# A hybrid bidirectional encoder on one core: scan products moved from GpSimd to VectorE, attention's one-column operations in per-row scalar form, output weights split in quarters

## The chip, the cores and the metric

The kernel runs on one core of a Trainium2 chip. A core has TensorE (matmuls; PE in the profile, PEld for its weight loads), VectorE (DVE), ScalarE (ACT), GpSimd (POOL) and SyncE (SP, which here only issues DMAs), and 16 DMA engines between SBUF and device memory. Each engine works through its own instructions in order and meets the others only at semaphores. The metric is the device time of the program in microseconds (us); lower is better.

## The reference, cut to what matters

Two layers over a sequence of 2048 rows of 1024 numbers. A layer normalises, projects to 4128 columns, feeds three head groups, gates each, concatenates, projects back and adds the residual:

```python
for layer in range(DEPTH):                      # DEPTH = 2
    h = rms_norm(x, norm_pre[layer])
    proj = h @ w_in[layer]
    y_a = gla_branch(...)    # gated linear attention, both directions
    y_b = diff_branch(...)   # differential softmax attention, 4 heads
    y_c = hgrn_branch(...)   # gated linear recurrence, both directions
    y = jnp.concatenate([y_a, y_b, y_c], axis=-1) @ w_out[layer]
    x = x + rms_norm(y, norm_post[layer])

def block(qblk):                                # one block of 128 queries of diff_branch
    s = jnp.einsum('cbhqd,cbhkd->cbhqk', qblk, k)
    p = jax.nn.softmax(s, axis=-1)
    w = p[0] - lam * p[1]
    return jnp.einsum('bhqk,bhkv->bhqv', w, v)

def step(state, inp):                           # the recurrence in y_a and y_c
    g_n, u_n = inp
    return g_n[..., None] * state + u_n, state
```

All arithmetic is float32; large matmuls are made of split operands (a rounded high part and the low remainder).

## The kernel before, in words

A layer has three stages. In the **input projection** TensorE makes all 4128 columns, in 18 blocks of at most 288 columns (`first` and `rest`), each first for rows 0 to 1023 (part 0), then for rows 1024 to 2047 (part 1). Its matmuls write PSUM tiles named `pp` (lines 297 and 306). Weights come through GpSimd's DMA queue (`wraw`, line 214) and are split into `whi` and `wlo`.

During part 1 the **scans** of the two recurrences run between the projection blocks: 12 groups a layer (`scan_group`: three head pairs by four stretches of 512 rows). A group goes through seven levels. At each it multiplies half of the keys `kt` by the gate products of the level below (line 617, on GpSimd), half of the queries `qt` by them (line 619, VectorE), and makes the gate products `nt` of the next level (line 625, GpSimd; 512, 256, ... 8 columns). From level 3 ScalarE first copies keys and queries into the layout that TensorE reads (`kc`, `qc`, `kp`, `qp`), and VectorE puts the products into `att` (line 613). `near` (line 545) makes the products of the lowest levels on VectorE, and line 638 sums them after a transpose (`pd`). The order of this whole stage is not written out: a planner of the framework sets it from its own costs, with the scans at a raised priority. When the last group is done its memory goes to the attention, whose first loads (`aq`, `aga`, `ks`, `vt`) stand in the queues of SP and GpSimd and wait for that.

The **attention** runs 64 units a layer (4 heads by 16 blocks of 128 queries) in an order written out by hand: a loop over frames `f`, four frames to a unit, in which `at_lag(lag, name, k)` emits a step of the unit that began `lag` frames earlier. On VectorE a unit is:

- four `maxima` (line 878, over 1024 scores each), the second followed by the minimum of two columns (line 881);
- `sums` (895), `sums2` (899 and 900), `lows` (891), `total` (904, with its sum written out as a second instruction), `inverse` (908), `factors` (912), all on one or two columns;
- two `combine` (line 916, 1024 columns from two SBUF tiles).

Beside it run on GpSimd, in turn: at the start of the attention a chain of 28 pairs of state updates (lines 775 and 778); from unit 16 on the `Inter` steps; from unit 50 on the split of the output weights (`load_wo`, lines 792 and 794, one of eight row blocks per unit); and throughout the gate products (950, 951) and the query split (730, 732). The order on every engine is that of the calls, for instance:

```python
at_lag(4, "lows", 0)
at_lag(6, "combine", 0, 0)
at_lag(6, "combine", 2, 1)
at_lag(5, "total", 0)
at_lag(3, "sums", 0)
at_lag(0, "maxima")
at_lag(5, "inverse", 0)
at_lag(3, "sums2", 0)
at_lag(5, "factors", 0)
```

The **output projection** (line 1038) follows, with the next layer's normalisation beside it.

Of the kernel before, what the change touches and what calls it, by code (L numbers as in the profile page):

```python
# [11 lines left out]
F32 = mybir.dt.float32  # L12
# [48 lines left out]
def tile_hybrid_encoder(  # L61
# [178 lines left out]
    for l in range(DEPTH):  # L240
# [15 lines left out]
        with ExitStack() as s1:  # L256
# [243 lines left out]
            def scan_group(ti, g, tot):  # L500
# [91 lines left out]
                for lev in range(1, 8):  # L592
# [23 lines left out]
                    ka = custom(kt, 0, [(512 + h, 2), (2 * h, n2), (1, h)])  # L616
                    nc.gpsimd.tensor_tensor(ka, ka, custom(tt, toff + 1, [(tn - 1, 2), (2, n2), (0, h)]), op=ALU.mult)  # L617
                    qa = custom(qt, h, [(512 - h, 2), (2 * h, n2), (1, h)])
# [4 lines left out]
                    else:  # L623
                        nto = tot[:, :, 4 * g:4 * g + 4]
                    nc.gpsimd.tensor_tensor(nto, custom(tt, toff, [(tn, 2), (2, n2)]),
                                            custom(tt, toff + 1, [(tn, 2), (2, n2)]), op=ALU.mult)
# [128 lines left out]
        with ExitStack() as s2:  # L755
# [27 lines left out]
            def load_wo():  # L783
                ow = s2.enter_context(tc.tile_pool(name=f"ow{l}", bufs=1, side="right"))
                raws = wr_st.enter_context(tc.tile_pool(name=f"wr{l}", bufs=1, side="right"))
                npost.append(ow.tile([P, D], F32, name="npost"))
                nc.sync.dma_start(npost[0], norm_post[l:l + 1].to_broadcast([P, D]))
                for k in range(KC):
                    raw = raws.tile([P, D], F32, tag="woraw", name="woraw", bufs=2)
                    nc.sync.dma_start(raw, w_out[l, k * P:(k + 1) * P, :])  # L790
                    hi = ow.tile([P, D], F32R, name=f"wohi{k}")
                    nc.gpsimd.tensor_copy(hi, raw)
                    lo = ow.tile([P, D], F32R, name=f"wolo{k}")
                    nc.gpsimd.tensor_tensor(lo, raw, hi.bitcast(F32), op=ALU.subtract)
                    wo_hi.append(hi)
                    wo_lo.append(lo)
                    yield
# [51 lines left out]
            class Unit:  # L849
# [26 lines left out]
                def maxima(self, k):  # L876
# [3 lines left out]
                    if k == 1:  # L880
                        nc.vector.tensor_tensor(mx[:, 4:5], mx[:, 0:1], mx[:, 1:2], op=ALU.min)

# [7 lines left out]
                def lows(self):  # L890
                    nc.vector.tensor_tensor(self.mx[:, 5:6], self.mx[:, 2:3], self.mx[:, 3:4], op=ALU.min)

                def sums(self):
                    gm, sm = self.gm, self.sm
                    nc.vector.tensor_tensor(gm[:, 2:3], sm[:, 0:1], sm[:, 1:2], op=ALU.add)

# [5 lines left out]
                def total(self):  # L902
                    gm, sm = self.gm, self.sm
                    nc.vector.scalar_tensor_tensor(gm[:, 6:8], gm[:, 4:6], 1.0, sm[:, 2:4], op0=ALU.mult, op1=ALU.mult,
                                                   accum_out=gm[:, 0:1])

                def inverse(self):
                    nc.vector.reciprocal(self.gm[:, 0:1], self.gm[:, 0:1])

                def factors(self):  # L910
                    gm = self.gm
                    nc.vector.tensor_scalar(gm[:, 8:10], gm[:, 4:6], gm[:, 0:1], gm[:, 1:2], op0=ALU.mult, op1=ALU.mult)

# [42 lines left out]
            with tc.manual_schedule(engines={getattr(mybir.EngineType, e) for e in ENGINES}):  # L956
                for f in range(4 * NU + 13):
# [24 lines left out]
                    at_lag(7, "transposes")  # L982
                    at_lag(4, "lows", 0)
                    at_lag(6, "combine", 0, 0)
                    at_lag(6, "combine", 2, 1)
                    at_lag(5, "total", 0)
                    at_lag(3, "sums", 0)
                    at_lag(0, "maxima")
                    at_lag(5, "inverse", 0)
                    at_lag(3, "sums2", 0)  # L990
                    at_lag(5, "factors", 0)
                    at_lag(8, "copy")
# [135 lines left out]
```

## Time and profile before

| what | us |
| --- | --- |
| median of three runs (3727.11 to 3730.25) | 3727.13 |
| the profiled execution | 3726.52 |
| its span, first to last instruction | 3724.7 |
| TensorE busy | 3542.4 (95%) |
| VectorE busy | 2556.2 (69%) |
| GpSimd busy | 1726.8 (46%) |

The span is cut into stages by lines: in layer one the scans lie at about 400 to 882 us, the rest of the input projection up to 1017, the attention from there to about 1660, the output projection to about 1870; layer two repeats this from there. A view of windows gives, for a stretch, the busy time of each engine and the granted TensorE clock. A view of lines groups the instructions of one source line. A timeline has one instruction a row, start and duration; a VectorE record and the next one's can overlap by some 0.08 us, so what an instruction takes out of a full queue is the distance to the next start.

### The profile page before, as it was taken

The numbers are of one execution on the slowest core, as the hardware profiler recorded it, in microseconds if no ns is written. First come the engines' busy times: TensorE is split into PE (matmuls) and PEld (weight loads), VectorE is DVE, ScalarE is ACT, GpSimd is POOL, SyncE is SP. The second block draws the span as 40 slices with busy tenths as digits, with TensorE's granted clock in tenths as the row PEclk, the third lists the DMA queues.
The fourth block names the chain that finished last, engine by engine and source line by source line (L and its number), as shares of the span: only waits on it lengthen the run. The fifth ranks groups of instructions, "written<-read, shape, count | busy, mean of one in ns | idle before, by whom it ended". The sixth has DMA issues, their size and how long they took to land.

```text
span 3724.7 us, 62216 instructions
## 1 busy us (share of the span) xinstructions
PE 3542.4 (95%) x23296; PEld 3162.7 (85%) x23296; DVE 2556.2 (69%) x3962; ACT 1929.1 (52%) x4340; POOL 1726.8 (46%) x1694
## 2 busy tenths in 40 slices
PE   8999999999989999899989999999999899998999
PEld 7898988897878999788888989878878789997887
DVE  5422778884499999985324237888834999999733
ACT  4521545541377888774225115554413778887722
POOL 3545644444475665520035456443434856664200
PEclk9999999999999999999999999999999999999999
DMA  5444444445341332214334434444453413322143
GB/s 157 129 137 135 136 136 141 139 122 165 106 127 38 116 115 82 66 40 134 119 110 143 130 126 140 139 137 139 112 182 101 115 38 121 118 75 67 38 136 113
DMA packets 293645, 430.49 MB, mean 116 GB/s; under 512 B 42400, under 2 KB 185312, under 8 KB 291040
## 3 DMA queue, kind: packets, MB, share of 16 engines
q1 hardware_dynamic: 268896, 333.71, 29.0%
q0 software_dynamic: 22336, 90.71, 8.3%
q8 instruction: 184, 3.01, 0.3%
q10 hardware_dynamic: 2112, 2.10, 0.2%
q14 instruction: 117, 0.96, 0.1%
HBM read 275.82 MB, written 152.57 MB: 115 GB/s over the span
## 4 chain that ended last, share of the span: by engine, by line
PE 58%; DVE 23%; DMA 9%; issue 4%; POOL 3%; ACT 2%; SPq 1%; DVEq 0%; POOLq 0%; ACTq 0%
PE pp L306 13%; PE pp L297 9%; PE pob L1038 9%; PE po L933 8%; DVE mx L878 5%; PE s L873 4%; PE s L874 4%; PE pt L922 4%; DVE e L916 3%; DMA wraw<-in_w_in_dram 3%; DVE pr L545 2%; DVE att L613 2%; DVE qt L619 2%; DMA cs<-c_rope 2%; PE poi L823 1%
## 5 line engine op out<-in xcount | busy, mean ns | idle before, releaser
L887 ACT ACTIVATE e<-s,mx 128x1024 f32<-128x1024 f32 x512 | 571.0, 1119 | 154.7 <-DVE mx L878 112.1
L878 DVE TENSOR_REDUCE mx<-s 128x1 f32<-128x1024 f32 x512 | 621.3, 1215 | 36.1 <-PE s L874 35.9
L306 PE MATMUL pp<-wlo,hhi 128*128 128x256 f32 (+1 forms) x2048 | 590.8, 288 | 5.4 <-POOL wlo L224 5.4
L306 PE MATMUL pp<-whi,hhi 128*128 128x256 f32 (+1 forms) x2048 | 587.8, 287 | 8.2 <-DVE ru L335 7.1
L306 PE MATMUL pp<-whi,hlo 128*128 128x256 f32 (+1 forms) x2048 | 592.3, 289 | 0.5 <-DVE hlo L195 0.5
L933 PEld LDWEIGHTS po<-vt,wt 128*128 128x128 f32 x4096 | 532.7, 191 | 70.6 <-ACT o L940 30.9
L933 PE MATMUL po<-vt,wt 128*128 128x128 f32 x4096 | 544.4, 276 | 17.4 <-ACT o L940 17.4
L873 PE MATMUL s<-ks,aqh 128*128 128x512 f32 x1024 | 450.4, 440 | 28.3 <-ACT e L887 27.2
L297 PE MATMUL pp<-hhi,whi 128*128 128x512 f32 x1024 | 412.4, 403 | 15.2 <-DVE ru L335 15.2
L297 PE MATMUL pp<-hlo,whi 128*128 128x512 f32 x1024 | 411.8, 402 | 0.0
L297 PE MATMUL pp<-hhi,wlo 128*128 128x512 f32 x1024 | 411.0, 401 | 0.0
L874 PE MATMUL s<-ks,aql 128*128 128x512 f32 x1024 | 403.9, 394 | 2.0 <-POOL aql L732 2.0
L306 PEld LDWEIGHTS pp<-whi,hhi 128*128 128x128 f32 x2048 | 393.4, 192 | 11.1 <-issue 8.4
L306 PEld LDWEIGHTS pp<-wlo,hhi 128*128 128x128 f32 x2048 | 391.7, 191 | 7.0 <-POOL wlo L224 6.1
L306 PEld LDWEIGHTS pp<-whi,hlo 128*128 128x128 f32 x2048 | 392.2, 192 | 3.4 <-DVE hlo L195 0.7
L916 DVE SCALAR_TENSOR_TENSOR e<-e,gam 128x1024 f32<-128x1024 f32 x256 | 370.8, 1449 | 4.5
L926 ACT COPY wt<-pt 128x512 f32<-128x512 f32 x512 | 301.2, 588 | 97.8 <-PE pt L922 96.2
L922 PE MATMUL pt<-ident,e 128*128 128x128 f32 x2048 | 310.7, 274 | 17.3 <-DVE e L916 10.2
L617 POOL TENSOR_TENSOR kt<-kt,nt 128x512 f32<-128x512 f32 x144 | 197.9, 1378 | 201.8 <-ACT kc L579 96.7
L214 POOL DMA_DIRECT2D wraw<-in_w_in_dram x124 | 97.0, 782 | 367.7 <-DVE sso L1045 183.6
L922 PEld LDWEIGHTS pt<-ident,e 128*128 128x128 f32 x2048 | 238.2, 141 | 27.4 <-issue 13.7
L873 PEld LDWEIGHTS s<-ks,aqh 128*128 128x128 f32 x1024 | 194.8, 190 | 61.1 <-ACT e L887 36.8
(190 smaller groups left out, 7301.4 us busy)
## 6 DMA issues: line engine op xcount, KB each, us to landing
wraw<-in_w_in_dram POOLq DMA_DIRECT2D x116, 512.0 KB, 5.0
cs<-c_rope SPq DMA_DIRECT2D x32, 512.0 KB
dr_gate<-z SPq DMA_DIRECT2D x64, 256.0 KB
aq<-dr_q SPq DMA_DIRECT2D x256, 64.0 KB
ks<-dr_k POOLq DMA_DIRECT2D x16, 1024.0 KB, 7.8
y<-dr_y SPq DMA_DIRECT2D x32, 512.0 KB
dr_qs<-qt SPq DMA_DIRECT2D x48, 256.0 KB
qs<-dr_qs SPq DMA_DIRECT2D x24, 512.0 KB
```

The lines of the kernel that those rows point to most:

```text
L297: nc.tensor.matmul(ps.rearrange("p (a t) -> p a t", t=P), w[a][:, k, c:c + P], b[g][:, :, k], start=n == 0, stop=n == 3 * KC - 1)
L306: nc.tensor.matmul(ps, b[g][:, t % 4, k], w[a][:, k, :n], start=cnt == 0, stop=cnt == 3 * KC - 1)
L617: nc.gpsimd.tensor_tensor(ka, ka, custom(tt, toff + 1, [(tn - 1, 2), (2, n2), (0, h)]), op=ALU.mult)
L873: nc.tensor.matmul(s[:, i], self.qh[:, c, js], kk, start=True, stop=False)
L874: nc.tensor.matmul(s[:, i], self.ql[:, c, js], kk, start=False, stop=True)
L878: nc.vector.tensor_reduce(mx[:, k:k + 1], self.s[k].rearrange("p a n -> p (a n)"), axis=AX.X, op=ALU.max, negate=True)
L887: nc.scalar.activation(self.es[c][:, n * 1024:(n + 1) * 1024], self.s[kk].rearrange("p a n -> p (a n)"), AF.Exp, bias=self.mx[:, m:m + 1], ...
L916: nc.vector.scalar_tensor_tensor(es[0][:, hs], es[1][:, hs], gm[:, 8 + n:9 + n], es[0][:, hs], op0=ALU.mult, op1=ALU.add)
L922: nc.tensor.transpose(pt[:, i], self.es[0][:, (4 * q + i) * P:(4 * q + i + 1) * P], ident)
L926: nc.scalar.copy(wt, self.pt[q])
L933: nc.tensor.matmul(self.po, self.wt[q][:, i], self.v[:, k], start=k == 0, stop=k == NT - 1)
L1038: nc.tensor.matmul(pos[:, n], a[:, k], b[k][:, n * 512:(n + 1) * 512], start=cnt == 0, stop=cnt == 3 * KC - 1)
```

## The change

Four edits.

1. In the scan, lines 617 and 625 are issued on VectorE instead of GpSimd, with the same operands.
2. In the attention, the operations on two one-column tensors (lines 881, 891, 895) become `tensor_scalar` with the second column as a per-row scalar. `total` becomes two such instructions (a product, then product and sum) in place of one with a written-out sum. `factors` becomes two instructions of one column each, the second in the next frame just ahead of `combine`.
3. `load_wo` splits each row block in four quarters of 256 columns: copy and subtract, four times.
4. What the planner then does with the input projection, and with the queues around it, moves as well.

```diff
-                    nc.gpsimd.tensor_tensor(ka, ka, custom(tt, toff + 1, [(tn - 1, 2), (2, n2), (0, h)]), op=ALU.mult)
+                    nc.vector.tensor_tensor(ka, ka, custom(tt, toff + 1, [(tn - 1, 2), (2, n2), (0, h)]), op=ALU.mult)
...
-                    nc.gpsimd.tensor_tensor(nto, custom(tt, toff, [(tn, 2), (2, n2)]),
+                    nc.vector.tensor_tensor(nto, custom(tt, toff, [(tn, 2), (2, n2)]),
...
-                    nc.gpsimd.tensor_copy(hi, raw)
...
-                    nc.gpsimd.tensor_tensor(lo, raw, hi.bitcast(F32), op=ALU.subtract)
+                    for n in range(4):
+                        cols = slice(n * D // 4, (n + 1) * D // 4)
+                        nc.gpsimd.tensor_copy(hi[:, cols], raw[:, cols])
+                        nc.gpsimd.tensor_tensor(lo[:, cols], raw[:, cols], hi[:, cols].bitcast(F32), op=ALU.subtract)
...
-                        nc.vector.tensor_tensor(mx[:, 4:5], mx[:, 0:1], mx[:, 1:2], op=ALU.min)
+                        nc.vector.tensor_scalar(mx[:, 4:5], mx[:, 0:1], mx[:, 1:2], None, op0=ALU.min)
...
-                    nc.vector.tensor_tensor(self.mx[:, 5:6], self.mx[:, 2:3], self.mx[:, 3:4], op=ALU.min)
+                    nc.vector.tensor_scalar(self.mx[:, 5:6], self.mx[:, 2:3], self.mx[:, 3:4], None, op0=ALU.min)
...
-                    nc.vector.tensor_tensor(gm[:, 2:3], sm[:, 0:1], sm[:, 1:2], op=ALU.add)
+                    nc.vector.tensor_scalar(gm[:, 2:3], sm[:, 0:1], sm[:, 1:2], None, op0=ALU.add)
...
-                    nc.vector.scalar_tensor_tensor(gm[:, 6:8], gm[:, 4:6], 1.0, sm[:, 2:4], op0=ALU.mult, op1=ALU.mult,
-                                                   accum_out=gm[:, 0:1])
+                    nc.vector.tensor_scalar(gm[:, 6:7], gm[:, 4:5], sm[:, 2:3], None, op0=ALU.mult)
+
+                def total2(self):
+                    gm, sm = self.gm, self.sm
+                    nc.vector.tensor_scalar(gm[:, 0:1], gm[:, 5:6], sm[:, 3:4], gm[:, 6:7], op0=ALU.mult, op1=ALU.add)
...
-                    nc.vector.tensor_scalar(gm[:, 8:10], gm[:, 4:6], gm[:, 0:1], gm[:, 1:2], op0=ALU.mult, op1=ALU.mult)
+                    nc.vector.tensor_scalar(gm[:, 8 + n:9 + n], gm[:, 4 + n:5 + n], gm[:, 0:1], gm[:, 1:2], op0=ALU.mult, op1=ALU.mult)
```

On VectorE in the attention, one unit before, from its last maxima to the next unit's second (line numbers after 789 differ by up to five between the two kernels):

```order
L878 TENSOR_REDUCE mx<-s 128x1
L899 TENSOR_SCALAR gam<-gam,neglam 128x1
L900 TENSOR_SCALAR gam<-gam 128x1
L891 TENSOR_TENSOR mx<-mx 128x1
L916 SCALAR_TENSOR_TENSOR e<-e,gam 128x1024
L878 TENSOR_REDUCE mx<-s 128x1
L904 SCALAR_TENSOR_TENSOR gam<-gam,sm 128x2
L878 TENSOR_REDUCE mx<-s 128x1
L881 TENSOR_TENSOR mx<-mx 128x1
L908 RECIPROCAL gam<-gam 128x1
L912 TENSOR_SCALAR gam<-gam 128x2
L916 SCALAR_TENSOR_TENSOR e<-e,gam 128x1024
```

The same place after:

```order
L880 TENSOR_REDUCE mx<-s 128x1
L901 TENSOR_SCALAR gam<-gam,neglam 128x1
L902 TENSOR_SCALAR gam<-gam 128x1
L893 TENSOR_SCALAR mx<-mx 128x1
L921 SCALAR_TENSOR_TENSOR e<-e,gam 128x1024
L880 TENSOR_REDUCE mx<-s 128x1
L906 TENSOR_SCALAR gam<-gam,sm 128x1
L910 TENSOR_SCALAR gam<-gam,sm 128x1
L880 TENSOR_REDUCE mx<-s 128x1
L883 TENSOR_SCALAR mx<-mx 128x1
L913 RECIPROCAL gam<-gam 128x1
L917 TENSOR_SCALAR gam<-gam 128x1 x2
```

No place in the row changes; the forms do, and of a unit's instructions only the two `combine` still read two tensors from SBUF.

On VectorE in the scans of layer one, before, inside a pair of levels:

```order
L545 TENSOR_TENSOR pr<-kt,qt 128x128x2 x4
L619 TENSOR_TENSOR qt<-qt,nt 128x2x4x64
L613 COPY_PREDICATED att<-masks,pm 128x2x256 x2
L619 TENSOR_TENSOR qt<-qt,nt 128x2x128x2
L321 SCALAR_TENSOR_TENSOR lsm<-zg,lse 128x512
```

A like place after:

```order
L625 TENSOR_TENSOR nt<-nt 128x32
L613 COPY_PREDICATED att<-masks,pm 128x2x256 x2
L617 TENSOR_TENSOR kt<-kt,nt 128x2x128x2
L619 TENSOR_TENSOR qt<-qt,nt 128x2x128x2
L613 COPY_PREDICATED att<-masks,pm 128x2x256 x2
L619 TENSOR_TENSOR qt<-qt,nt 128x2x4x64
L617 TENSOR_TENSOR kt<-kt,nt 128x2x4x64
L441 COPY zh<-pp 128x512
L625 TENSOR_TENSOR nt<-gt 128x512
```

Each product of the queries now has one of the keys beside it in VectorE's own queue, and GpSimd's queue holds nothing but weight loads between the gate block and the first `ru` of the key blocks. In TensorE's order the last scan matmul of a layer (`pu`, line 680) stood behind 3798 of the layer's 4608 `pp` matmuls; it now stands behind 3974, while the first `pd` stands behind 2443 before and 2427 now.

In SP's queue at the end of the scans, before (`aq` and `aga` are the attention's first loads, `cs` the rotary table of a key or query block, of which the kernel holds one at a time):

```order
L345 DMA dr_k<-rh 4x32x512
L728 DMA aq<-dr_q 32x2x256
L346 DMA dr_k<-ru 4x32x512
L728 DMA aq<-dr_q 32x2x256 x3
L734 DMA aga<-dr_gate 128x2x128
L728 DMA aq<-dr_q 32x2x256 x4
L734 DMA aga<-dr_gate 128x2x128 x2
L345 DMA dr_k<-rh 4x32x512
L330 DMA cs<-c_rope 128x2x512
L346 DMA dr_k<-ru 4x32x512
```

After:

```order
L330 DMA cs<-c_rope 128x2x512
L340 DMA dr_q<-ru 4x32x512 x2
L662 DMA dr_oi<-oi 128x4x128
L699 DMA dr_u<-ut 64x3x128
L699 DMA dr_u<-ut 64x4x128
L728 DMA aq<-dr_q 32x2x256 x3
L340 DMA dr_q<-ru 4x32x512
L330 DMA cs<-c_rope 128x2x512
L728 DMA aq<-dr_q 32x2x256
L734 DMA aga<-dr_gate 128x2x128
L728 DMA aq<-dr_q 32x2x256 x4
L734 DMA aga<-dr_gate 128x2x128 x2
```

Before, four loads of `cs` stand behind the first `aq` of a layer; now one does.

## Rows read from the trace of the kernel before

**Rows 1.** The page's chain that ended last, shares of the span by engine:

```profile
PE 58%; DVE 23%; DMA 9%; issue 4%; POOL 3%; ACT 2%; SPq 1%; DVEq 0%; POOLq 0%; ACTq 0%
```

**Rows 2.** Windows of layer one: stretch and length, busy us of each engine, PEclk, DMA.

```profile
400.00:840.00 440.00, 417.77 (x2992) 377.25 (x2991) 370.86 (x583) 221.85 (x485) 205.65 (x199) 0.96 0.46 135
840.00:1017.00 177.00, 166.50 (x1063) 148.12 (x1063) 70.32 (x100) 41.59 (x68) 79.73 (x65) 0.96 0.44 135
1051.00:1142.00 91.00, 78.34 (x511) 67.82 (x511) 89.00 (x119) 62.21 (x144) 87.36 (x76) 0.98 0.23 73
1259.00:1415.00 156.00, 155.86 (x1118) 143.93 (x1117) 148.18 (x241) 131.26 (x312) 96.59 (x131) 1.00 0.35 109
1493.00:1580.00 87.00, 76.64 (x516) 66.68 (x515) 86.15 (x120) 61.93 (x146) 44.69 (x41) 1.00 0.23 71
1619.00:1654.00 35.00, 35.00 (x249) 32.22 (x248) 32.99 (x60) 30.34 (x72) 6.11 (x10) 1.00 0.04 12
```

**Rows 3.** Timeline, attention without GpSimd work: start us, duration us, instruction.

```profile
1629.33 0.20 DVE L899 TENSOR_SCALAR gam<-gam,neglam 128x1 f32<-128x1 f32 x1
1629.45 0.19 DVE L900 TENSOR_SCALAR gam<-gam 128x1 f32<-128x1 f32 x1
1629.58 0.14 DVE L891 TENSOR_TENSOR mx<-mx 128x1 f32<-128x1 f32 x1
1629.64 1.27 DVE L916 SCALAR_TENSOR_TENSOR e<-e,gam 128x1024 f32<-128x1024 f32 x1
...
1633.56 0.29 DVE L912 TENSOR_SCALAR gam<-gam 128x2 f32<-128x2 f32 x1
```

**Rows 4.** Timeline, attention while GpSimd splits output weights:

```profile
1531.07 2.38 POOL L794 TENSOR_TENSOR wolo<-woraw,wohi 128x1024 fp32r<-128x1024 f32 x1
1531.10 2.37 DVE L912 TENSOR_SCALAR gam<-gam 128x2 f32<-128x2 f32 x1
1533.50 1.28 DVE L916 SCALAR_TENSOR_TENSOR e<-e,gam 128x1024 f32<-128x1024 f32 x1
```

**Rows 5.** VectorE by line, 1051 to 1142: count, busy us, mean ns, idle before.

```profile
L916 DVE SCALAR_TENSOR_TENSOR e<-e,gam 128x1024 f32<-128x1024 f32 x16 | 27.1, 1696 | 0.3
L912 DVE TENSOR_SCALAR gam<-gam 128x2 f32<-128x2 f32 x8 | 7.9, 987 | 0.3
L891 DVE TENSOR_TENSOR mx<-mx 128x1 f32<-128x1 f32 x8 | 6.0, 748 | 0.0
L881 DVE TENSOR_TENSOR mx<-mx 128x1 f32<-128x1 f32 x8 | 5.0, 622 | 0.3
L904 DVE SCALAR_TENSOR_TENSOR gam<-gam,sm 128x2 f32<-128x2 f32 x8 | 4.0, 505 | 0.0
L895 DVE TENSOR_TENSOR gam<-sm 128x1 f32<-128x1 f32 x7 | 4.0, 566 | 0.0
L900 DVE TENSOR_SCALAR gam<-gam 128x1 f32<-128x1 f32 x8 | 1.6, 198 | 0.0
```

**Rows 6.** VectorE by line, 1493 to 1580:

```profile
L916 DVE SCALAR_TENSOR_TENSOR e<-e,gam 128x1024 f32<-128x1024 f32 x16 | 26.0, 1623 | 0.3
L912 DVE TENSOR_SCALAR gam<-gam 128x2 f32<-128x2 f32 x8 | 10.7, 1337 | 0.3
L895 DVE TENSOR_TENSOR gam<-sm 128x1 f32<-128x1 f32 x8 | 8.4, 1050 | 0.0
```

**Rows 7.** VectorE by line in the scans, 400 to 840:

```profile
L619 DVE TENSOR_TENSOR qt<-qt,nt 128x512 f32<-128x512 f32 x69 | 61.2, 892 | 8.0 <-ACT qc L581 7.0 <-ACT qp L558 0.8
...
L545 DVE TENSOR_TENSOR pr<-kt,qt 128x256 f32<-128x256 f32 x48 | 17.5, 421 | 0.0
```

**Rows 8.** Line 619 over the whole trace, shortest/median/longest ns:

```profile
L619 DVE TENSOR_TENSOR qt<-qt,nt x144: 664/692/2036, 426.3 to 2714.8; 128x512 f32<-128x512 f32 x144
```

**Rows 9.** TensorE's waits, 400 to 1016: us, times, longest.

```profile
PE pp L297 <- DVE ru L335: 7.4, 1, 7.4
```

**Rows 10.** Timeline of SP's issues at the end of the scans (start, duration):

```profile
895.56 11.62 SPq L728 DMA_DIRECT2D aq<-dr_q  x4
```

More of the change, by code (lines that the diff above doesn't have):

```diff
@@ L903, in total, with factors @@
                     gm, sm = self.gm, self.sm
-                    nc.vector.scalar_tensor_tensor(gm[:, 6:8], gm[:, 4:6], 1.0, sm[:, 2:4], op0=ALU.mult, op1=ALU.mult,
-                                                   accum_out=gm[:, 0:1])
+                    nc.vector.tensor_scalar(gm[:, 6:7], gm[:, 4:5], sm[:, 2:3], None, op0=ALU.mult)
+                def total2(self):
+                    gm, sm = self.gm, self.sm
+                    nc.vector.tensor_scalar(gm[:, 0:1], gm[:, 5:6], sm[:, 3:4], gm[:, 6:7], op0=ALU.mult, op1=ALU.add)
                 def inverse(self):
                     nc.vector.reciprocal(self.gm[:, 0:1], self.gm[:, 0:1])
-                def factors(self):
+                def factors(self, n):
                     gm = self.gm
-                    nc.vector.tensor_scalar(gm[:, 8:10], gm[:, 4:6], gm[:, 0:1], gm[:, 1:2], op0=ALU.mult, op1=ALU.mult)
+                    nc.vector.tensor_scalar(gm[:, 8 + n:9 + n], gm[:, 4 + n:5 + n], gm[:, 0:1], gm[:, 1:2], op0=ALU.mult, op1=ALU.mult)
                 def combine(self, n):
@@ L983, in tile_hybrid_encoder @@
                     at_lag(4, "lows", 0)
+                    at_lag(6, "factors", 0, 1)
                     at_lag(6, "combine", 0, 0)
@@ L987, in tile_hybrid_encoder @@
                     at_lag(3, "sums", 0)
+                    at_lag(5, "total2", 0)
                     at_lag(0, "maxima")
@@ L990, in tile_hybrid_encoder @@
                     at_lag(3, "sums2", 0)
-                    at_lag(5, "factors", 0)
+                    at_lag(5, "factors", 0, 0)
                     at_lag(8, "copy")
```

## The prediction

> **What bounds the kernel now.** I read the chain first, then the windows, then single lines inside the windows in which TensorE isn't full. The chain runs through TensorE for 58% and through VectorE for 23% of the span [rows 1]: two engines share the end, and the windows say where. In the middle of the attention (1259 to 1415) TensorE is busy 155.86 of 156 us; nothing that VectorE saves there can be had. In two other stretches of the attention it is not: 1051 to 1142, with TensorE at 78.34 of 91 and VectorE at 89.00, and 1493 to 1580, with 76.64 of 87 and 86.15 [rows 2]. There VectorE sets the pace. In the scans (400 to 840) both are loaded, TensorE 417.77 and VectorE 370.86 of 440, and TensorE's clock is granted at 0.96 on average, so in a part of the stretch at its lower level, 1.2 instead of 2.4 GHz [rows 2]. Layer two shows the same stages, and I price each once and double it.
>
> Why is VectorE slow in the two stretches? The work per unit is the same as at 1619, where nothing is slow. With GpSimd idle, a one-column `tensor_tensor` takes 0.14 us and the next starts 0.06 later; line 912 takes 0.29 [rows 3]. While GpSimd subtracts a weight block for 2.38 us, line 912 takes 2.37: it starts just behind, ends with it, and only then does line 916 run, in its plain 1.28 [rows 4]. So an instruction with two SBUF tensors, or line 912, waits until GpSimd's current one is done. Lines 899 and 900, with a per-row scalar on one column, keep 198 ns in the busiest stretch [rows 5], and have 0.19 to 0.20 us in the quiet one [rows 3]. That is the whole ground for edit 2.
>
> **The attention's first stretch, GpSimd's state updates.** Nine small instructions a unit take some 32 us over 8 units: the five lines that sum to 27 us and line 900's 1.6 in [rows 5], and three like the last or smaller; with the overlap of 0.08 us off seven of them, 3.4 us a unit. After: nine per-row-scalar instructions at the 0.12 from one start to the next of line 899 [rows 3], one reciprocal, and about 0.35 for the three places where one needs the result of the one ahead (`total2`, the minimum, the first factor): 1.4, or 1.7 if two scalars cost the 0.09 that line 912 takes over line 899. That removes 2.0 us a unit. Two parts don't come home. The wait of `lows` (748 against 140 ns, 0.6) only moves: `combine` stands right behind it and would have met the same GpSimd instruction. And `combine` keeps its own wait, now 1696 against 1280, 0.83 a unit; without line 912 holding GpSimd off just ahead, it meets it at a random point, half of some 1.2 us, so 0.6, a gain of 0.2. Net 1.6 us of 11.4 (91 us for 8 units); between 1.0, with a full GpSimd instruction ahead of each `combine`, and 2.4, with none. The pace stays above TensorE's, 8.7 us a unit at 1619 (35 us for four units, TensorE full). The 28 pairs of updates cover about 9 units: **-14 us** a layer (-9 to -22).
>
> **The second stretch, the output weights.** Line 912 waits 1337 - 290 and line 895 1050 - 140, together 1.95 us a unit; some 0.3 more lies on line 881, and the new forms cost 0.35 on top of the old ones' plain price: -1.9. The quarters act on what is left. `combine` pays 1623 - 1280, 0.7 a unit for two [rows 6], behind pieces of up to 2.38 us [rows 4]; behind pieces of about a quarter, 0.6, it pays some 0.3. That gives -2.3 of 11.2, but TensorE's 8.7 to 9.2 is near: I take -2.0 over 8 units, **-16 us** a layer (-10 to -19). The quarters lengthen GpSimd's own row by start costs only, and nothing waits for the weights before line 1038.
>
> Elsewhere in the attention the new forms add 0.35 us to VectorE's unit. It is hidden: at 1619 VectorE has 32.99 of 35 and would have 34.4. Without that cover it costs 0.3 on a dozen units, 4 us a layer; I take 1.
>
> The Trainium skill (VectorE: DVE Perf Modes, "The TRN2 errata") prices a VectorE instruction from SBUF at 58 cycles plus its columns, so about 0.06 us for any one-column form. The 0.06 after line 891 agrees; the 0.12 after line 899 is double. By the page the new forms would cost 0.12 a unit instead of 0.35, an estimate of 8 us less over the two stretches of both layers; the row decides.
>
> **The scan.** VectorE takes over 84 key products a layer at the plain time of line 619, 0.66 to 0.69 us [rows 8], 57 us, and 84 gate products: the largest near 0.68, the next two near 0.4 (line 545) [rows 7], the last four 0.15 to 0.4; 12 x 2.3 = 27. With the overlap off, +72. It gets back the waits that these very instructions caused on GpSimd: line 619 runs 892 on average [rows 7] against 664 at its shortest [rows 8], 81 x 0.22 = 18; line 545, 144 times some 0.09, 12; lines 528, 645 and 223 some 5 more: -35. Net **+37 us of VectorE work a layer** on 371 of 440. If all of it showed, that is the bound above. But the planner spreads it: the scan's last matmuls move behind 176 more projection matmuls, into a stretch where VectorE has 70 of 177 [rows 2], and TensorE has projection work to fill with. So it costs TensorE nothing as long as its order fits, and the plan fits better when VectorE's times aren't stretched by waits. What can go are gaps: above all the 7.4 us that TensorE waits for line 335 [rows 9], whose table `cs` stands in SP's queue behind attention loads that hold it for 11.62 us from 895.56 on [rows 10]; small ones, behind `dg` and others, are spread over the scans. One load of `cs` stands there after the change instead of four. I take -8 for this gap and the slow clock behind it and -2 for the rest: **-10** a layer (-57, if all of the 33 us idle and of the lost clock, 617 x 0.04 = 24 us, between 400 and 1017 went [rows 2], to +37). The attention's loads come some 60 us later, still ahead of the last projection block.
>
> **Sum.** 2 x (-14 - 16 + 1 - 10) = -78. From the execution's 3726.5 that is 3648.5; the median lies 0.6 above it: **3649 us**.
>
> **Rivals.**
> *VectorE becomes the bound of the scan* (slower). For: VectorE's 23% of the chain [rows 1], its place ahead of `dg`, and 408 of 440 us if nothing moved. Against: the wider spread. It decides from about 95% of the stretch on; then the 37 us show in both layers: -58 + 74, 3743.
> *The waits move on to `combine`.* For: `lows` shows how. Against: line 895 and 881 are followed by instructions that don't wait. Half the attention's gain stays: -29 - 20, 3678.
> *The per-row forms wait as well*, so edit 2 does nothing. Line 912 speaks for it, a `tensor_scalar` that waits; but it has two columns, and lines 899 and 900 with one never do. Only quarters and scan are left, and 0.35 x 34 units is added: -6 + 12 - 20, 3713. The Trainium skill (SBUF — State Buffer, "Who interferes with whom") names `tensor_scalar` among those that can take the pair of ports shared with GpSimd, if their shape allows it; line 912 agrees, line 899 doesn't.
> *The scan's gaps go too*: half of 57 a layer instead of 10: -58 - 57, 3612.
>
> **How the numbers follow.** Forecast 0.63, with its own range 3625 to 3672; combine 0.15; gaps 0.10; scan bound 0.08; forms wait 0.04. The range of 8 in 10 takes in the third and most of the second: 3612 to 3695. This kernel can be told from no change from about 0.2% on, 7.5 us. Faster: the first three and half of the last, 0.90; slower, most of the scan case, 0.06; same 0.04.
>
> **What would show it.** Lines 883, 893, 897, 906, 910 and 917 near 0.2 us whatever GpSimd does; units of 9.5 to 10 us in the first stretch, near 9 in the second; 9.75 in the middle as before. In the scan, the new line 617 near 0.68 and line 619 near its shortest; TensorE's gaps no larger than now; no wait for line 335 above some 3 us. Wrong it would be if `combine` grew towards 2.4 us in the first stretch, if VectorE passed 95% of the scans, or if the attention's first loads came too late for its first unit.

## The result and the profile after

The changed kernel takes 3634.88 us (median of four runs, 3629.27 to 3641.44) beside 3727.12 for the kernel before on the same chip: ratio 0.9753, 95% interval 0.9734 to 0.9773. That is faster, 14 us below the forecast of 3649 and inside its range. The sum was nearly right, but by luck: three of its four terms were off by 5 to 12 us a layer, and their errors cancel.

The profiled execution took 3641.44 us, the longest of the four and 85.1 less than the 3726.52 of the one before. First the page's chain by engine and the windows of layer one, cut at the places that answer to [rows 1, 2] (stretch and length, busy us of PE, PEld, DVE, ACT, POOL, granted clock, DMA share, GB/s):

```profile
PE 67%; DVE 13%; DMA 10%; POOL 4%; issue 3%; ACT 1%; SPq 1%; DVEq 0%; POOLq 0%; ACTq 0%
```

```profile
400.00:840.00 440.00, 425.90 (x3044) 385.67 (x3043) 396.03 (x732) 221.19 (x481) 56.83 (x50) 0.98 0.49 143
840.00:997.00 157.00, 148.62 (x1039) 134.13 (x1039) 79.45 (x120) 44.52 (x74) 57.80 (x48) 0.97 0.44 134
1033.00:1121.00 88.00, 79.33 (x512) 70.70 (x511) 75.61 (x129) 62.70 (x144) 84.36 (x74) 0.92 0.22 67
1159.00:1468.00 309.00, 309.00 (x2234) 287.18 (x2234) 293.54 (x513) 260.79 (x623) 210.31 (x259) 1.00 0.33 100
1469.00:1543.00 74.00, 72.52 (x509) 65.93 (x508) 72.98 (x127) 61.54 (x144) 57.92 (x81) 1.00 0.27 84
```

VectorE left the chain (23% to 13%) and TensorE took its place. Eight units of the second stretch, with the output weights, now last 74 us instead of 87, and TensorE is busy in 72.52 of them. Eight units of the first stretch, with the state updates, still last 88 instead of 91: VectorE's busy time fell from 89.00 to 75.61, TensorE's stayed (78.34 and 79.33), and its clock went down to 0.92. GpSimd is busy 84.36 of 88.

VectorE's instructions with the new forms and `combine` in six units of that first stretch, 1050 to 1121, by line (count, busy us, mean ns, idle before):

```profile
L921 DVE SCALAR_TENSOR_TENSOR e<-e,gam 128x1024 f32<-128x1024 f32 x13 | 22.9, 1761 | 0.0
L917 DVE TENSOR_SCALAR gam<-gam 128x1 f32<-128x1 f32 x12 | 2.7, 269 | 0.2
L910 DVE TENSOR_SCALAR gam<-gam,sm 128x1 f32<-128x1 f32 x6 | 1.6, 273 | 0.2
L883 DVE TENSOR_SCALAR mx<-mx 128x1 f32<-128x1 f32 x6 | 1.3, 214 | 0.2
L897 DVE TENSOR_SCALAR gam<-sm 128x1 f32<-128x1 f32 x6 | 1.2, 199 | 0.0
```

None of the new forms waits for GpSimd: 0.20 to 0.27 us where [rows 5] had 0.5 to 1.0 (the two that are not in these rows, lines 893 and 906, have 0.20). What did not go is the wait of `combine`: 1761 ns here, 1696 in [rows 5].

The products in the scans of layer one, on VectorE, as in [rows 7]:

```profile
L617 DVE TENSOR_TENSOR kt<-kt,nt 128x512 f32<-128x512 f32 x64 | 44.6, 700 | 1.2 <-ACT kc L579 1.1
L619 DVE TENSOR_TENSOR qt<-qt,nt 128x512 f32<-128x512 f32 x64 | 44.6, 697 | 0.0
...
L625 DVE TENSOR_TENSOR nt<-nt 128x256 f32<-128x256 f32 (+4 forms) x58 | 17.8, 308 | 0.2
L625 DVE TENSOR_TENSOR nt<-gt 128x512 f32<-128x512 f32 x12 | 8.2, 685 | 0.0
```

Line 619 fell from 892 to 697 ns, and line 617 has 0.70, as forecast from [rows 8]. TensorE's wait of [rows 9], at line 297, is gone; for line 335 it waits only at line 306, in the last of these rows (TensorE's five longest waits from the scans to the first scores: us, times, longest):

```profile
PE po L658 <- DVE dg L638: 5.1, 2, 4.9
PE pd L637 <- issue: 3.5, 1, 3.5
PE pm L587 <- ACT qc L581: 2.8, 2, 2.2
PE pm L587 <- DVE dg L638: 2.4, 2, 1.5
PE pp L306 <- DVE ru L335: 2.2, 1, 2.2
```

That smaller wait was there before too, beside the one of [rows 9]:

```profile
PE pp L306 <- DVE ru L335: 2.3, 1, 2.3
```

By stage, from the profiled executions (layer one / layer two, us). "Scan" runs from the first `pd` transpose (line 637) to the attention's first scores, so it holds the rest of the input projection; the units are cut at the first scores matmul of each:

| | scan | units 0-15 | units 16-47 | units 48-63 |
| --- | --- | --- | --- | --- |
| before | 593.0 / 594.5 | 162.5 / 163.3 | 314.0 / 314.0 | 160.6 / 160.7 |
| after | 571.8 / 572.7 | 161.5 / 158.9 | 309.9 / 309.9 | 146.7 / 146.4 |
| mean difference | -21.5 | -2.7 | -4.1 | -14.1 |
| forecast | -10 | -14 | +1 | -16 |

The differences sum to -42.4 a layer, so -84.8 of the -85.1. The second stretch is right. The first gave next to nothing, the scan twice what I took, and the middle something where I had a small loss. The last two make up for the first: that the total came out is luck.

In the scan, the windows of before and after show two parts (same columns; both layers of before, then both of after):

```profile
423.90:1016.90 593.00, 563.93 (x3882) 505.20 (x3883) 423.82 (x660) 256.67 (x542) 269.25 (x249) 0.96 0.44 132
2278.90:2873.40 594.50, 559.44 (x3882) 500.87 (x3882) 427.66 (x661) 256.54 (x543) 269.47 (x249) 0.97 0.44 131
```

```profile
425.50:997.30 571.80, 552.75 (x3898) 498.24 (x3898) 458.91 (x824) 257.74 (x542) 104.38 (x89) 0.98 0.46 137
2238.20:2810.90 572.70, 554.55 (x3897) 500.30 (x3897) 459.27 (x825) 258.36 (x543) 104.53 (x89) 0.97 0.46 137
```

TensorE's idle time, length less busy time, fell from 29 and 35 us to 19 and 18. Its busy time fell by 11 and 5 us too, although the stage now holds 16 more matmuls; in layer one the granted clock rose from 0.96 to 0.98 with it, so less of the stretch ran at the lower of its two levels, 1.2 instead of 2.4 GHz. VectorE's busy time rose by 32 to 35.

### The profile page after: what moved, and what is told of

Read it like the earlier page. It is cut to its first block, busy times and chain, and to the rows that moved or that the text cites. A ratio compares the mean times of both kernels' runs of the same rounds, so it can differ in the third digit from the quotient of the medians.

```text
span 3639.6 us, 62254 instructions
## 1 busy us (share of the span) xinstructions
PE 3513.4 (97%) x23296; PEld 3159.5 (87%) x23296; DVE 2560.3 (70%) x4426; ACT 1927.8 (53%) x4340; POOL 1459.6 (40%) x1454
## 3 DMA queue, kind: packets, MB, share of 16 engines
q1 hardware_dynamic: 268896, 333.71, 29.7%
## 4 chain that ended last, share of the span: by engine, by line
PE 67%; DVE 13%; DMA 10%; POOL 4%; issue 3%; ACT 1%; SPq 1%; DVEq 0%; POOLq 0%; ACTq 0%
PE pp L306 14%; PE pp L297 12%; PE pob L1045 10%; PE po L938 9%; PE s L875 5%; PE s L876 5%; PE pt L927 5%; DMA wraw<-in_w_in_dram 3%; DVE mx L880 3%; DMA cs<-c_rope 2%; PE pm L587 2%; DVE e L921 2%; PE pm L568 1%; DMA ust<-dr_u 1%; PE poi L825 1%
## 5 line engine op out<-in xcount | busy, mean ns | idle before, releaser
L889 ACT ACTIVATE e<-s,mx 128x1024 f32<-128x1024 f32 x512 | 571.7, 1121 | 74.8 <-DVE mx L880 53.3
L876 PE MATMUL s<-ks,aql 128*128 128x512 f32 x1024 | 407.2, 398 | 14.2 <-POOL aql L732 14.1
L921 DVE SCALAR_TENSOR_TENSOR e<-e,gam 128x1024 f32<-128x1024 f32 x256 | 392.3, 1533 | 0.0
L297 PEld LDWEIGHTS pp<-hhi,whi 128*128 128x128 f32 x1024 | 194.6, 190 | 45.0 <-issue 0.9
```

Of the source, the lines that this page charges most:

```text
L297: nc.tensor.matmul(ps.rearrange("p (a t) -> p a t", t=P), w[a][:, k, c:c + P], b[g][:, :, k], start=n == 0, stop=n == 3 * KC - 1)
L876: nc.tensor.matmul(s[:, i], self.ql[:, c, js], kk, start=False, stop=True)
L889: nc.scalar.activation(self.es[c][:, n * 1024:(n + 1) * 1024], self.s[kk].rearrange("p a n -> p (a n)"), AF.Exp, bias=self.mx[:, m:m + 1], ...
L921: nc.vector.scalar_tensor_tensor(es[0][:, hs], es[1][:, hs], gm[:, 8 + n:9 + n], es[0][:, hs], op0=ALU.mult, op1=ALU.add)
```

## The edits apart

The first question is which edit brought what. Four kernels start from the kernel before. The products on VectorE alone (edit 1):

```diff
-                    nc.gpsimd.tensor_tensor(ka, ka, ...
+                    nc.vector.tensor_tensor(ka, ka, ...
...
-                    nc.gpsimd.tensor_tensor(nto, ...
+                    nc.vector.tensor_tensor(nto, ...
```

> The kernel before with edit 1 alone: both products by gates on VectorE, nothing else. Theory A (the projection's 43 us of gain in the full change come from edit 1 alone, 21 us a layer between the first pd and the first score): 3727 - 43 = 3684, the attention's units as before (11.2 to 11.6 us in the first stretch, 10.5 and 11.2 in the second). Rival B (what the scan gained came from the new order of SP's and GpSimd's queues that only the full change has): above 3700.

The one-column forms alone (edit 2: `tensor_scalar` for `tensor_tensor`, `total2`, and `factors` by columns):

```diff
-                        nc.vector.tensor_tensor(mx[:, 4:5], mx[:, 0:1], mx[:, 1:2], op=ALU.min)
+                        nc.vector.tensor_scalar(mx[:, 4:5], mx[:, 0:1], mx[:, 1:2], None, op0=ALU.min)
...
```

> The kernel before with edit 2 alone: per-row-scalar forms in the attention, output weights whole, scan products on GpSimd. Theory A (the small operations' waits are what edit 2 removes, but the first stretch has GpSimd as its next bound, and the second keeps combine's wait behind whole weight pieces): second stretch from 10.9 to about 9.6 us a unit, first stretch down by no more than 0.4, middle 9.68, so 3727 - 25 = 3702. Rival B (VectorE alone set the first stretch's pace): first stretch below 10 us a unit and 3685 or less. Rival C (the waits only move to combine): combine's mean in the second stretch from 1.62 to above 2.2 us and 3720.

The quarters alone (edit 3):

```diff
-                    nc.gpsimd.tensor_copy(hi, raw)
+                    for n in range(4):
+                        cols = slice(n * D // 4, (n + 1) * D // 4)
+                        nc.gpsimd.tensor_copy(hi[:, cols], raw[:, cols])
...
```

> The kernel before with edit 3 alone: output weights split in quarters. Theory A (a wait lasts as long as GpSimd's current instruction, so shorter pieces shorten every wait): line 912 in the second stretch from 1.34 to about 0.6 us, units there from 10.9 to about 9.7, 3727 - 18 = 3709; the first stretch unchanged. Rival B (waits add up to the same, since there are more pieces to meet): 3725.

Forms and quarters together, both of these diffs in one kernel:

> Edits 2 and 3 together, scan products left on GpSimd. Theory A (attention and projection gain apart from each other): 3727 - 42 = 3685, with the attention as in the full change (second stretch 9.3 us a unit, first stretch 11.0). Rival B (the two edits gain less together than apart, since TensorE's 9.1 to 9.2 us a unit is reached by either alone): then e2 and e3 alone sum to clearly more than this one.

| kernel | us | ratio to before | scan | units 0-15 | 16-47 | 48-63 |
| --- | --- | --- | --- | --- | --- | --- |
| edit 1 | 3675.18 | 0.9856 (0.9835 to 0.9876) | 569.1 / 568.5 | 161.3 / 162.6 | 315.1 / 313.9 | 160.6 / 160.9 |
| edit 2 | 3699.55 | 0.9928 (0.9904 to 0.9951) | 587.3 / 595.2 | 159.8 / 159.4 | 309.9 / 309.9 | 151.4 / 151.4 |
| edit 3 | 3701.51 | 0.9926 (0.9908 to 0.9945) | 590.2 / 595.1 | 163.0 / 162.6 | 313.8 / 313.9 | 147.1 / 148.1 |
| edits 2 and 3 | 3687.08 | 0.9887 (0.9868 to 0.9907) | 594.2 / 590.5 | 160.0 / 160.1 | 309.9 / 309.9 | 146.7 / 146.6 |

(us are medians; the kernel before had 3726.85 beside them; stages as in the table above.) Edit 1 gives 52 us and edits 2 and 3 together 40; the sum, 92, is the whole change. The scan and the attention gain apart. Edits 2 and 3 don't: alone they give 27 and 25, together 13 less than that, since both act on units 48 to 63. (Where the scan isn't edited, it still reads 587.3 to 595.2 us; a difference of up to 8 us in that column says nothing.)

Two readings go against my working. In units 48 to 63 the quarters alone give 13 of the 14 us, the forms alone 9: I had given the forms 1.9 of 2.3 us a unit and let the quarters "act on what is left". VectorE's lines in that stretch with the old forms and the new quarters show why:

```profile
L918 DVE SCALAR_TENSOR_TENSOR e<-e,gam 128x1024 f32<-128x1024 f32 x16 | 21.5, 1342 | 0.3
L914 DVE TENSOR_SCALAR gam<-gam 128x2 f32<-128x2 f32 x8 | 7.1, 890 | 0.3
L897 DVE TENSOR_TENSOR gam<-sm 128x1 f32<-128x1 f32 x7 | 4.0, 574 | 0.0
```

Against [rows 6] all three waits shrank with GpSimd's pieces (a subtraction takes 1.04 us on average instead of 2.38, a copy 0.43 instead of 1.47): `combine` 1623 to 1342, the factors 1337 to 890, line 897 (895 of before) 1050 to 574. With the forms alone `combine` rose to 1934 ns there:

```profile
L919 DVE SCALAR_TENSOR_TENSOR e<-e,gam 128x1024 f32<-128x1024 f32 x16 | 30.9, 1934 | 0.0
```

The waits that the forms avoid come up again in the instruction behind them. That rival was real, and it was the quarters that kept it small.

And the middle's 4.1 us come from edit 2 alone: over units 16 to 47 a unit went from 9.81 to 9.68 us, although the window of [rows 2] had TensorE busy in 155.86 of 156 us. Over all 32 units it was busy in 312.72 of 314.0, so 1.3 us were open gaps. A part of the rest stood inside records that count as busy. The 128-column `poi` matmuls of the `Inter` steps, four to a pair of units, over 240 us of the middle, before and after:

```profile
L823 PE MATMUL poi<-ust,qs 128*128 128x128 f32 x48 | 8.4, 298 | 0.1
```

```profile
L825 PE MATMUL poi<-ust,qs 128*128 128x128 f32 x52 | 7.9, 275 | 0.0
```

Four times 23 ns is 0.09 us a pair of units; a pair away from the longer ones went from 19.49 to 19.36. What held these matmuls isn't shown.

## Why the first stretch gave nothing: GpSimd's own queue

In units 4 to 11 after the change, VectorE is idle a seventh of the time and TensorE a tenth. TensorE's waits there:

```profile
PE s L876 <- POOL aql L732: 7.1, 2, 4.3
```

and one of them in the timeline (start us, duration us, idle before in brackets):

```profile
1052.47 0.60 POOL L730 CAST aqh<-aq 128x512 fp32r<-128x512 f32 x1
1053.06 3.47 POOL L778 TENSOR_TENSOR ust<-ust,st 64x512 f32<-64x512 f32 x2
...
1056.60 1.26 POOL L732 TENSOR_TENSOR aql<-aq,aqh 128x512 fp32r<-128x512 f32 x1
...
1057.92 0.80 PE L876 MATMUL s<-ks,aql 128*128 128x512 f32 x1 [4.29 <-POOL aql L732]
...
1059.61 1.23 DVE L880 TENSOR_REDUCE mx<-s 128x1 f32<-128x1024 f32 x1 [4.21 <-PE s L876]
```

The scores of a pair of units need `aql`, the low part of the queries, and that subtraction stands in GpSimd's row behind two state additions of 3.47 us in all. TensorE waits 4.29 us, VectorE behind it 4.21. Theory: GpSimd's in-order row sets this stretch, and the VectorE time that edit 2 frees can't be had. The rival: VectorE's remaining waits, `combine`'s above all, set it. Three kernels start from the kernel after. Half the columns of the state chain:

```diff
-                    nc.gpsimd.tensor_tensor(ust[rows, c + sh], ust[rows, c + sh], tmp[rows], op=ALU.add)
+                    nc.gpsimd.tensor_tensor(ust[rows, c + sh, 0:256], ust[rows, c + sh, 0:256], tmp[rows, 0:256], op=ALU.add)
...
```

> The kernel after, with the chain of state updates (multiply and add on GpSimd) on half of its 512 columns; the other half of the states is left out. Theory A, GpSimd's own row sets the attention's first stretch (10.7 of 11.2 us a unit busy, and the query's split waits in it): GpSimd loses some 4 us a unit, units 4 to 11 of each layer go from 11.0 to 9.3-9.8 us, attention from 618 to 602-606, the whole to 3600-3612. Theory B, VectorE's pace with its waits on GpSimd sets it: combine's wait for a shorter instruction falls by at most 0.4 us a unit, units stay above 10.4, the whole at 3625 or above.

The query's split off GpSimd in the first 16 units, the rounding to ScalarE and the subtraction to VectorE:

```diff
-                nc.gpsimd.tensor_copy(qh, qr)
...
-                nc.gpsimd.tensor_tensor(ql, qr, qh.bitcast(F32), op=ALU.subtract)
...
+                        split_q(*split_of[self.h, self.qb // 2], nc.scalar.copy, nc.vector)
```

> The kernel after, with the split of the query block (rounded high part, and the rest) for the first 16 units of head 0 done by ScalarE and VectorE instead of GpSimd. Theory A, the scores wait because the split stands in GpSimd's row behind the state updates: with it gone, GpSimd's row is 9.4 us a unit, nobody on TensorE's path waits for it, units 4 to 15 go from 10.5 on average to 9.3-9.8, 10-14 us a layer, the whole to 3607-3617. Theory B, VectorE sets the pace: it has 0.4 us a unit more to do and a subtraction with two inputs that waits for GpSimd, so units stay at 11 or rise, the whole to 3635-3650.

The state chain paced:

```diff
-            for i in range(14):
-                for d in range(2):
+            def states():
+                for i in range(14):
+                    for d in range(2):
...
+                        yield
...
+                    if 9 <= f < 65 and f % 2:
+                        next(st_it)
```

> The kernel after, with the 28 pairs of state updates written into the attention's order one pair every half unit from unit 2 to unit 15, instead of as early as GpSimd can; nothing is left out. Theory A, GpSimd's full row sets the attention's first stretch, by whatever stands in it (the query's split, or with that gone the output's gate): with 2 pairs a unit GpSimd has some 7.5 us a unit of work, nobody waits for it, units 4 to 11 go from 11.0 to 9.2-9.6 us and units 12 to 15 to 9.3-9.6, 10-14 us a layer, the whole at 3605-3617. Theory B, VectorE's waits on the same 56 instructions set it: they are met as often, only later, units 4 to 15 keep their sum (125.8 us), the whole at 3630-3642.

| kernel | us | ratio to before | us per unit, 4-7, 8-11, 12-15 (layer one) | units 0-15 |
| --- | --- | --- | --- | --- |
| after | 3634.88 | 0.9753 (0.9734 to 0.9773) | 11.20, 10.88, 9.38 | 161.5 / 158.9 |
| half the chain | 3622.09 | 0.9709 (0.9692 to 0.9727) | 11.30, 9.17, 9.01 | 151.6 / 151.4 |
| query's split moved | 3630.66 | 0.9730 (0.9711 to 0.9749) | 9.48, 11.60, 9.10 | 155.9 / 158.1 |
| chain paced | 3616.33 | 0.9707 (0.9677 to 0.9737) | 10.06, 9.48, 9.02 | 150.7 / 146.8 |

Half the chain doesn't make a unit faster while it runs (11.30); it is over sooner. So what hurts is that the queue is full: whatever its length, the chain is issued as early as GpSimd can take it, and everything behind it waits. Neither of the two expectations put it so, and the time missed both of their figures, 3600 to 3612 and 3625 or more. Moving the query's split cures units 4 to 7 (9.48) and hands the wait to the next one in the row, in units 8 to 11 (11.60). TensorE's and ScalarE's waits there (the output's gate, `aga`, is line 965 in that kernel):

```profile
PE po L948 <- ACT o L955: 6.8, 4, 2.2
```

```profile
ACT o L955 <- POOL aga L965: 9.1, 4, 3.1
```

ScalarE can't copy out the next result while GpSimd hasn't read the last but one, and TensorE waits for ScalarE. The time is not told apart from that of the kernel after. Pacing the chain, one pair every half unit up to unit 15, takes out nothing and moves nothing to another engine. The window of units 4 to 11 with it:

```profile
1026.90:1105.00 78.10, 76.24 (x512) 69.08 (x512) 71.44 (x124) 60.48 (x139) 74.29 (x65) 0.96 0.24 75
```

GpSimd's busy share is as before, 74.29 of 78.10 (I had expected 7.5 us a unit, not 9.3), though these eight units now hold some 17 of the 28 pairs instead of 23. TensorE's waits are down to this:

```profile
PE s L879 <- POOL aqh L730: 2.5, 1, 2.5
PE s L879 <- ACT e L893: 1.0, 2, 0.6
PE s L880 <- POOL aql L732: 0.8, 1, 0.8
```

Units 0 to 15 fall by 11 and 12 us; from the kernel before to this one it is 14 on average, the figure that I had forecast for the forms alone. The rival has a part in it, since `combine` waits less too. Over units 4 to 11 of the kernel after and of this one:

```profile
L921 DVE SCALAR_TENSOR_TENSOR e<-e,gam 128x1024 f32<-128x1024 f32 x16 | 27.9, 1746 | 0.0
```

```profile
L925 DVE SCALAR_TENSOR_TENSOR e<-e,gam 128x1024 f32<-128x1024 f32 x15 | 23.8, 1584 | 0.0
```

Of the 10 us that these units lose, TensorE's open gaps fell by 7 (8.67 to 1.86), while VectorE's busy time fell by 4 (75.61 to 71.44). The theory holds in this form: the order of GpSimd's row set the stretch, and its busy share did not. Whether pacing would have gained as much without the new forms, no run shows.

A fourth kernel asked whether `factors` by columns was needed; it has the two-column form again:

```diff
-                    nc.vector.tensor_scalar(gm[:, 8 + n:9 + n], gm[:, 4 + n:5 + n], gm[:, 0:1], gm[:, 1:2], op0=ALU.mult, op1=ALU.mult)
+                    nc.vector.tensor_scalar(gm[:, 8:10], gm[:, 4:6], gm[:, 0:1], gm[:, 1:2], op0=ALU.mult, op1=ALU.mult)
```

> The kernel after, with the two factors again in one tensor_scalar over two columns, as before, instead of two of one column. Theory A, the two-column form waits for GpSimd and the one-column form does not: its line takes 0.29 us where GpSimd is idle, but 1 us and more on average in the second stretch (1469 to 1543), whose units go from 9.3 to 9.6-9.9, 3-5 us a layer, the whole to 3641-3650; combine's wait is partly paid there instead. Theory B, the width plays no part: the line keeps 0.3 us everywhere, VectorE saves 0.25 us a unit, the whole at 3628-3636.

It took 3634.74 us, ratio 0.9745 (0.9730 to 0.9761), so no difference from the kernel after. Its rows in the second stretch, and behind them the same two of the kernel after:

```profile
L921 DVE SCALAR_TENSOR_TENSOR e<-e,gam 128x1024 f32<-128x1024 f32 x16 | 22.3, 1394 | 0.3
L917 DVE TENSOR_SCALAR gam<-gam 128x2 f32<-128x2 f32 x8 | 6.7, 835 | 0.3
```

```profile
L921 DVE SCALAR_TENSOR_TENSOR e<-e,gam 128x1024 f32<-128x1024 f32 x16 | 26.1, 1629 | 0.0
L917 DVE TENSOR_SCALAR gam<-gam 128x1 f32<-128x1 f32 x16 | 3.6, 269 | 0.3
```

The two-column form waits, 835 ns, and the one-column form doesn't, as I read from [rows 4, 5]. But it is the same wait: it stands in front of `combine` or in it. 22.3 + 6.7 is 29.0 us, 26.1 + 3.6 is 29.7. Of edit 2 this part is worth nothing. The Trainium skill (SBUF — State Buffer, "Who interferes with whom") lets `tensor_scalar` take the pair of ports shared with GpSimd only in certain modes. The trace agrees in so far as one width waits (835 ns) and the other doesn't (269); no run here shows which mode either had.

## What the scan paid for

Edit 1 takes VectorE's waits on GpSimd away, and it also shortens the way through each level, which went to GpSimd and back. A kernel that brings the first back without the second: the kernel after, with a GpSimd product beside each key product that reads the same gates and whose result nobody uses.

```diff
+                    nc.gpsimd.tensor_tensor(custom(idle, 0, [(256, 2), (h, n2), (1, h)]), custom(idle, 0, [(256, 2), (h, n2), (1, h)]),
+                                            custom(tt, toff + 1, [(tn - 1, 2), (2, n2), (0, h)]), op=ALU.mult)
```

> The kernel after, plus one GpSimd instruction beside each key product on VectorE: it multiplies a private table that nobody uses by the same gates, with the same shapes as the key product that GpSimd had before. VectorE waits for none of its results. It tells apart why the scan lost 21 us a layer, from 594 to 572 from the first transposes to the first scores. Theory A, the waits that two-input VectorE instructions have while GpSimd works: these come back, VectorE's time above its shortest durations rises from 23 us towards the 49 of before in the scans, and the stage goes to 583-592 a layer, the whole to 3655-3670. Theory B, VectorE no longer has to wait for a result of GpSimd in each level: the extra instruction costs nothing, the stage stays at 570-577, the whole at 3633-3645.

It took 3729.67 us, ratio 0.9996 (0.9983 to 1.0009): as much as the whole change had brought is lost, for instructions on an engine that had time (POOL 230.69 of 616 us in the window):

```profile
430.40:1046.50 616.10, 581.01 (x3897) 520.64 (x3898) 498.87 (x824) 256.91 (x542) 230.69 (x169) 0.93 0.43 126
```

Against the kernel after, VectorE is busy 40 us more in this stage, for the same 824 instructions; TensorE is idle 35 us instead of 19, its clock 0.93 instead of 0.98. The stage costs 44 us more (39 in layer two). The direction is theory A's, the size more than twice what it said: I had put 26 us on VectorE's waits, which came out at 40, and nothing on the lower clock behind each gap: TensorE's busy time rose by 28. TensorE runs the same matmuls here in the same order as in the kernel after, so a new order of its work is no rival; VectorE's and SP's rows differ in a few neighbouring places. (In the next two kernels the planner lays TensorE's order anew, so a part of each difference can be the order; that wasn't taken apart.)

Then each product by itself. The gate products (line 625) back on GpSimd, the key products (617) on VectorE:

```diff
-                    nc.vector.tensor_tensor(nto, ...
+                    nc.gpsimd.tensor_tensor(nto, ...
```

> The kernel after, with the gate products (line 625) back on GpSimd; the key products (line 617) stay on VectorE. Theory A, VectorE's waits while GpSimd computes are what the scan paid for: before, 31.4 of 35.5 us of them fell beside line 617 and 4.1 beside line 625, so nearly all of the gain stays: 572-580 us a layer from the first transposes to the first scores, the whole at 3637-3655. Theory B, the way from VectorE to GpSimd and back in each level, by the gates that the next level needs, is what the scan paid for: it is there again, 584-594 us a layer, the whole at 3658-3680.

and the other way about:

```diff
-                    nc.vector.tensor_tensor(ka, ka, ...
+                    nc.gpsimd.tensor_tensor(ka, ka, ...
```

> The kernel after, with the key products (line 617) back on GpSimd; the gate products (line 625) stay on VectorE. Theory A, the waits beside line 617 (31.4 of 35.5 us before) are back: 588-598 us a layer from the first transposes to the first scores, the whole at 3668-3690. Theory B, the way by the gates is gone as in the kernel after: 570-578 us a layer, the whole at 3632-3648.

| kernel | us | ratio to before | scan |
| --- | --- | --- | --- |
| after (both on VectorE) | 3634.88 | 0.9753 (0.9734 to 0.9773) | 571.8 / 572.7 |
| only keys on VectorE | 3613.67 | 0.9695 (0.9673 to 0.9718) | 555.0 / 556.3 |
| only gates on VectorE | 3691.33 | 0.9905 (0.9883 to 0.9928) | - / 596.8 |

(In layer one of the last kernel the first scores stand ahead of a part of the projection, so that its stage can't be cut the same way.) With the gates alone on VectorE the scan is as slow as before; line 619 is at 921 ns again:

```profile
L619 DVE TENSOR_TENSOR qt<-qt,nt 128x512 f32<-128x512 f32 x72 | 66.1, 921 | 2.0 <-ACT qc L581 2.0
```

With the keys alone there, the scan is 17 us a layer faster than with both, better than either theory allowed. Whatever the trip to GpSimd and back by the gates costs, it is less than what the gate products cost on VectorE. The window of layer one:

```profile
427.20:982.10 554.90, 545.91 (x3904) 491.91 (x3905) 449.93 (x744) 255.93 (x542) 174.65 (x166) 0.99 0.48 141
```

TensorE is idle 9 us (19 with both) and busy 7 less. One execution of each is little for a size, but more kernels here share a scan. The six with both products on VectorE read 565.3 to 572.9 us a layer (mean 569.6), the two with the keys alone there 551.4 to 556.3 (554.3), the four with neither 587.3 to 595.2 (592.5). So the key products are worth some 38 us a layer, and the gate products on VectorE, with the order that the planner then lays, cost some 15 of it back: the -21.5 of the change is a gain and a loss.

## A version that is faster than both

The last kernel takes both findings: keys on VectorE, gates on GpSimd, and the state chain paced.

```diff
-                    nc.vector.tensor_tensor(nto, ...
+                    nc.gpsimd.tensor_tensor(nto, ...
...
+                    if 9 <= f < 65 and f % 2:
+                        next(st_it)
```

> The kernel after, with both edits that gained: the gate products (line 625) back on GpSimd, and the state updates written one pair every half unit. Theory A, they gain apart, one in the scan and one in the attention's first stretch: some 17 us a layer in the scan (555 instead of 572) and 11 us a layer in the attention (604-607 instead of 617), the whole at 3583-3597. Theory B, they share a bound, such as GpSimd's row at the border of the two stages: less than half of the second gain is added, the whole at 3603-3614.

It took 3587.53 us (five runs, 3584.97 to 3590.28), ratio to before 0.9616 (0.9599 to 0.9634). The scan takes 551.4 / 554.3 us and units 0 to 15 take 147.1 / 151.5: the two gains add, one in each stage. Between the kernel after and the one with the chain paced the intervals still touch (0.9734 and 0.9737); here the pacing is clear of noise, 0.9634 at most against 0.9673 at least with the keys alone, whose units 0 to 15 take 159.8 / 160.4.

## The prediction, point by point

**First stretch, -14 a layer: wrong, -2.7 measured.** The instructions did as forecast, 0.20 to 0.27 us each. The step that failed is "The pace stays above TensorE's": I looked only at whether TensorE would be the next bound. GpSimd stood at 87.36 of 91 us in [rows 2], and the queries' split and the output's gate are in its row, but I read that row only as the cause of VectorE's waits and not as a bound of its own. With the chain paced, the stage comes out at -14, and its units 4 to 11 take 9.8 us in layer one, inside the 9.5 to 10 that I had named as a sign; in the kernel after they take 11.0. Two slips did not matter here: TensorE's pace at 1619 is 9.0 us a unit and not 8.7, since a unit has 64 matmuls and the 35 us hold 249 of them, 3.9 units and not four; and the 1.4 us of the new forms leaves out the reciprocal, about 0.1.

**Second stretch, -16: right in size, -14.1, wrong in its parts.** Either edit alone gives most of it, the quarters 13. `combine` kept its 1629 ns, where I had it pay 0.3 us a unit; VectorE at 72.98 of 74 and TensorE at 72.52 are both full now, and that is where the stage ends. My "of 11.2" should have read 10.9 (87 us for eight units), so that -2.3 already led below TensorE's 9.0: the size came from that bound more than from the sum of the waits.

**Elsewhere, +1: wrong, -4.1.** I took a TensorE that is busy 155.86 of 156 us for one that can't be made faster. The price of the forms was right: at 1580 to 1615, with little GpSimd work, VectorE has 34.43 of 35, where I had said 34.4.

**Scan, -10: right in sign, too small; -21.5.** The price of the products was right (line 617 at 0.70; 32 to 35 us more on VectorE, where I had 37), and the wait of [rows 9] went as forecast, 7.4 us to none (SP's queue and TensorE's order changed together, so which of them did it isn't shown). The failed term is "-2 for the rest", with the 0.6 us that -8 left for the slow clock. TensorE's open gaps fell by 10.0 us in layer one, 2.6 beside that wait, and by 16.9 in layer two; its busy time fell by 11.2 and 4.9. How much of that clock belongs to which gap isn't shown. Wrong as well is "it costs TensorE nothing as long as its order fits": the gate products, 26 us for 70 of the 84 in the rows of line 625, cost some 15.

**Rivals.** The scan was not bound by VectorE as a whole (396.03 of 440, 90%), yet its added work was not free. The waits did move on to `combine` where the forms came alone. The per-row forms don't wait. The gaps went in part, 29 and 35 us to 19 and 18: for the scan this rival, at -28.5 a layer, was nearer than my -10, and the sum hid it.

## What to carry to other kernels

When VectorE waits for GpSimd, read GpSimd's row twice: as the cause of the waits, and as a queue in which something that TensorE needs may stand behind something that nobody needs yet. Where a long chain is issued as early as an engine can take it, pacing it can be worth more than making its neighbours immune. And of an edit that moves two things, time each alone: here one of them gained some 38 us a layer and the other lost some 15.

## What the runs showed that I had not expected

GpSimd instructions whose result nobody uses cost the stage more than they lengthened VectorE's records: 40 us of longer records in layer one became 44 us of the stage, TensorE's granted clock falling from 0.98 to 0.93 with the gaps. GpSimd is held up in its turn: one and the same form took 1.93 us in the kernel after where VectorE was in a `combine` until 1050.89, and 1.05 where VectorE was idle.

```profile
1049.19 1.70 DVE L921 SCALAR_TENSOR_TENSOR e<-e,gam 128x1024 f32<-128x1024 f32 x1
...
1049.88 1.93 POOL L775 TENSOR_TENSOR st<-ust,tst 64x512 f32<-64x512 f32 x1
...
1057.83 1.05 POOL L775 TENSOR_TENSOR st<-ust,tst 64x512 f32<-64x512 f32 x1
```

And a stretch in which TensorE reads as busy from end to end got shorter all the same: 0.09 us a pair of units stood inside records of its matmuls.
